# One layer of a hybrid encoder on one core: the seven products of an up-projection unit in a fixed order on TensorE

## The chip, the core and the metric

The kernel runs on one core of a Trainium2 chip. A core has five engines that run beside each other, each with a queue of its own: TensorE (matrix products; it writes to a memory of its own, PSUM, of eight banks), VectorE, ScalarE, GpSimd and SyncE (which issues most of the transfers). They wait for each other through semaphores. The metric is the time of one execution on the device in microseconds, lower is better.

## The reference

One layer works on 512 frames of a prompt and 64 frames of a sample, each a row of 2048 numbers. First come two recurrent mixers with their projections, then the feed-forward part, which is what matters here:

```python
def conv_ffn(h, st, w_up, ffn_conv_w, ffn_conv_b, w_down):
    gate, val = jnp.split(h @ w_up, 2, axis=-1)
    gate_c, new_st = causal_dwconv(gate, st, ffn_conv_w)
    act = jax.nn.silu(gate_c + ffn_conv_b) * val
    return act @ w_down, new_st
```

`w_up` is 2048 x 11264: 5632 gate columns and 5632 value columns. `causal_dwconv` is a convolution of width 3 along the frames. All arrays are float32.

## The kernel before

**The arithmetic.** A float32 product is made of three products of a shorter type: each weight block is split into `wh` (rounded, by ScalarE) and `wl` (the rest, by VectorE), each activation into `hi` and `lo`, and TensorE adds `wh*hi + wh*lo + wl*hi` in one PSUM bank.

**The up-projection.** It is cut into 44 units (`t`), each with 128 gate and 128 value columns. A unit is a 2 x 2 block product (gate and value by the two halves of the 2048 rows, against two halves of the frames), computed in Strassen's way with seven products (`c` = 0 to 6) in place of eight. The activations' combinations are made once, ahead of the stage. A product is 8 row blocks (`j`) times three matmuls of 128 x 128 weights by 290 columns: 24 matmuls into one bank (`up_product`, lines 1251 to 1263).

**The banks.** A unit takes a tile `g` of two banks and a tile `bank` of one (line 1255). The products go to x, y, z, x, y, z, y, where x and y are the banks of `g` and z is `bank`:

```python
        ps = self.banks[(0, 1, 2, 0, 1, 2, 1)[c]]
```

The products that come second and third to a bank add to what is there. Each product is read out as soon as it is done (`up_out`): c0 by ScalarE into `p1` (L1273); c1, c2, c3, c4 by VectorE (L1276, L1279, L1281, L1284); c5 and c6 by VectorE too (L1286 and L1287, L1291 and L1292).

**The weights.** `up_prep` prepares the weights of a product two products ahead: the sums that Strassen's way needs (`s1` L1219, `s2` L1228, L1238, L1243, 1.2 us each on VectorE) and the split (`wh` L1208 on ScalarE, `wl` L1209 on VectorE). Three pairs of split weights are kept, so a split begins when the product three before has released its pair. The raw blocks, 512 KB each, four a unit, come from DRAM by SyncE's queue into six buffers (`up_load`, L1202). After the gate's products its convolution runs on VectorE (L1311) and ScalarE (L1312), and the unit's result is multiplied (L1318) and written to DRAM (L1319). Two groups of VectorE's work, the convolution and the last multiplication, are already held behind the latest split with `issue_after`.

**The order.** No order of instructions is written out. The program is traced in the order of the loop in `up`, and a planner then runs it through a model of the engines: whenever an engine is free in the model, it issues the instruction that is ready there, the one traced first if there are several. What comes out is the fixed order of each engine's queue. `issue_after(ins)` adds an edge that holds for the order alone: what the block traces on `ins`'s engine is queued behind `ins`. It brings no semaphore.

Of the kernel before, what the change touches and what calls it, by code (L numbers as in the profile page):

```python
# [1 line left out]

# [1 line left out]

# [87 lines left out]
class Kern:  # L92
# [1158 lines left out]
    def up_product(self, t, c):  # L1251

        if c == 0:
            g = self.pgt()
            self.banks = g[:, 0, :HZ], g[:, 1, :HZ], self.bank()[:, :HZ]
        T, (wh, wl) = self.nc.tensor, self.a.pop((t, "w", c))
        ps = self.banks[(0, 1, 2, 0, 1, 2, 1)[c]]
        for j in range(NPAIR):
            hi, lo, _ = self.combos[c, j]

            T.matmul(ps, wh[:, j], hi, start=(c < 3 and j == 0), stop=False, skip_group_check=True)  # L1261
            T.matmul(ps, wh[:, j], lo, start=False, stop=False, skip_group_check=True)  # L1262
            T.matmul(ps, wl[:, j], hi, start=False, stop=(j == NPAIR - 1), skip_group_check=True)  # L1263

    def up_out(self, t, c):

        nc = self.nc
        V, A, G = nc.vector, nc.scalar, nc.gpsimd
        x, y, z = self.banks
        tmp = lambda n: self.ub.tile([P, HZ], F32, tag=n, name=self.name(n))  # L1270
        if c == 0:
            self.p1 = tmp("p1")
            A.activation(self.p1, x, AF.Copy)  # L1273
        elif c == 1:
            self.g = self.ub.tile([P, 2, HZ], F32, tag="g", name=self.name("g"))
            V.tensor_tensor(self.g[:, 1], y, self.p1, op=ALU.add)  # L1276
        elif c == 2:
            self.r = tmp("r")
            V.tensor_tensor(self.r, z, self.p1, op=ALU.add)  # L1279
        elif c == 3:  # L1280
            V.tensor_tensor(self.g[:, 0], x, self.rb[:, 0], op=ALU.mult)  # L1281
        elif c == 4:
            self.v = self.v_tile()
            V.tensor_tensor(self.v[:, 1], y, self.r, op=ALU.add)  # L1284
        elif c == 5:
            V.tensor_tensor(self.g[:, 1], z, self.g[:, 1], op=ALU.add)  # L1286
            V.tensor_tensor(self.g[:, 1], self.g[:, 1], self.rb[:, 1], op=ALU.mult)  # L1287
            self.up_gate(t, self.g)
        else:
            v = self.v  # L1290
            V.tensor_tensor(v[:, 0], y, self.p1, op=ALU.add)  # L1291
            V.tensor_tensor(v, v, self.rb, op=ALU.mult)  # L1292
# [33 lines left out]
    def up(self):  # L1326
        self.fs = self.cp.tile([P, 2, 2, NFF], F32, name="fs")
        self.cb = self.ub.tile([P, 2 * HZ], F32, tag="cb", name="cb")
        self.nc.gpsimd.tensor_copy(self.cb[:, 0:2], self.zero3[:, :2])
        self.up_state(0)  # L1330
        self.t2s = {}
        ahead = 2
        steps = [(t, c) for t in range(NFF) for c in range(7)]
        for n, (t, c) in enumerate(steps):
            if t == 0:
                for l in ((1,), (2,), (3,), (4,), (5, 6), (), ())[c]:
                    for j in range(N_EARLY, NPAIR):
                        self.pair_late(l, j)
            if n + ahead < len(steps):
                self.up_prep(*steps[n + ahead])  # L1340
            self.up_product(t, c)
            if n == 0:
                self.norm_end()

            if t > 0 and c == 0:
                with self.tc.issue_after(self.split_of):
                    self.up_conv(t - 1, self.ca)
                self.up_state(t)
            if t > 0 and c == 2:
                with self.tc.issue_after(self.split_of):  # L1350
                    self.up_act(t - 1, self.v, self.ca)
            self.up_out(t, c)
        self.up_conv(t, self.ca)
        self.up_act(t, self.v, self.ca)
# [291 lines left out]
```

## Time and profile before

| | us |
|---|---|
| median of 3 runs | 2995.6 (2995.07 to 3002.82) |
| the profiled execution | 3002.07 |
| its span, first to last instruction | 3000.3 |
| TensorE busy in the span | 2912.2 (97%) |
| VectorE busy | 2095.7 (70%) |
| ScalarE busy | 1242.9 (41%) |
| the up-projection, from its first matmul to its last | about 1020 |

How to read the rows further down. PE is TensorE, PEld its weight loads, DVE VectorE, ACT ScalarE, POOL GpSimd, SPq SyncE's queue. L1261 is line 1261 of the kernel. `g<-slot,wh` says that the instruction writes the tile `g` and reads the tiles `slot` and `wh`. A row of the timeline has the start, the duration, the engine, the line, the operation, the tiles, the shape, the count and, in brackets, the idle time of that engine before it and what ended it. A row of a window has its bounds and length, then the busy time and the number of instructions on PE, PEld, DVE, ACT and POOL (those engines that work in the windows asked for), the granted share of TensorE's clock, and the transfers' share and rate. Matmuls are pipelined: a row's duration is longer than the distance from one to the next.

### The profile page before, as it was taken

What the parts mean: (1) busy time and instruction counts of PE and PEld (TensorE: products, weight loads), DVE (VectorE), ACT (ScalarE), POOL (GpSimd) and SP (SyncE); (2) the same over time, 40 slices, a digit from 0 to 9 for tenths busy, and PEclk for the clock granted to TensorE, in tenths of its full rate; (3) what the DMA queues carried; (4) which work ended last, traced back from release to release, by engine and by line L of the source; (5) the groups of instructions that cost most, each with busy time, mean ns of one, the idle gap of its engine ahead of it and who ended that gap; (6) DMA issues with size and microseconds to landing.
All of it is one profiled execution on the core that took longest, in us unless ns stands there. A gap on an engine that the chain in (4) does not pass through costs nothing.

```text
span 3000.3 us, 52414 instructions
## 1 busy us (share of the span) xinstructions
PE 2912.2 (97%) x21128; PEld 2796.7 (93%) x21128; DVE 2095.7 (70%) x3226; ACT 1242.9 (41%) x2116; POOL 307.3 (10%) x610
## 2 busy tenths in 40 slices
PE   7988999999999999999999999999999999999998
PEld 3588899999999998999999999999999999999998
DVE  5776667776578777367888888888888865555555
ACT  6555444554343333255444444444444432212223
POOL 0033333332200000000000000000000000000000
PEclk9999999999999999999999999999999999999999
DMA  7844545554455456543333333333333473333221
GB/s 274 283 142 134 148 121 149 144 152 134 133 144 145 135 159 172 153 143 96 97 111 105 106 98 111 106 104 99 112 104 104 122 238 101 116 101 106 89 85 65
DMA packets 532599, 392.95 MB, mean 131 GB/s; under 512 B 58729, under 2 KB 463204, under 8 KB 532356
## 3 DMA queue, kind: packets, MB, share of 16 engines
q1 hardware_dynamic: 532356, 389.59, 43.5%
q8 instruction: 167, 2.74, 0.4%
q14 instruction: 76, 0.62, 0.1%
HBM read 355.16 MB, written 34.36 MB: 130 GB/s over the span
## 4 chain that ended last, share of the span: by engine, by line
PE 65%; DVE 2%; DMA 1%; ACT 1%; issue 1%; POOL 0%; SPq 0%; ACTq 0%; POOLq 0%; DVEq 0%
PE g L508 19%; PE g L510 10%; PE g L1261 8%; PE g L1262 8%; PE g L1263 8%; PE bank L1262 3%; PE bank L1261 3%; PE bank L1263 3%; PE bank L401 1%; DVE acc L738 0%; PE bank L140 0%; PE bank L744 0%; PE bank L1471 0%; POOL s L134 0%; DMA xr<-od 0%
## 5 line engine op out<-in xcount | busy, mean ns | idle before, releaser
L508 PE MATMUL g<-slot,wh 128*128 128x288 f32 x3168 | 551.9, 295 | 0.2 <-DVE slot L1031 0.2
L1261 PE MATMUL g<-slot,wh 128*128 128x290 f32 x1760 | 533.6, 303 | 2.4 <-ACT p L1273 2.4
L1262 PE MATMUL g<-slot,wh 128*128 128x290 f32 x1760 | 526.1, 299 | 0.0
L1263 PE MATMUL g<-slot,wl 128*128 128x290 f32 x1760 | 521.2, 296 | 0.0
L595 ACT ACTIVATE wh<-raw 128x1024 fp32r<-128x1024 f32 x223 | 235.4, 1058 | 613.6 <-PE g L508 596.7
L508 PEld LDWEIGHTS g<-slot,wh 128*128 128x128 f32 x3168 | 466.2, 188 | 0.7 <-DVE slot L1031 0.5
L508 PE MATMUL g<-hh,wh 128*128 128x288 f32 x1984 | 453.7, 307 | 1.9 <-DVE cb L881 1.5
L510 PE MATMUL g<-hh,wl 128*128 128x288 f32 x1984 | 443.9, 302 | 3.4 <-DVE wl L596 3.4
L508 PE MATMUL g<-hl,wh 128*128 128x288 f32 x1984 | 439.8, 301 | 0.0
L1031 DVE SCALAR_TENSOR_TENSOR slot<-g,mod,slot 128x512 f32<-128x512 f32 (+1 forms) x448 | 201.9, 492 | 308.9 <-PE g L510 304.7
L738 DVE SCALAR_TENSOR_TENSOR acc<-xr,ct,acc 128x512 f32<-128x512 f32 x480 | 340.0, 754 | 35.4 <-DMA xr<-in_w_ada_dram 34.8
L1208 ACT ACTIVATE wh<-raw 128x1024 fp32r<-128x1024 f32 x176 | 186.7, 1061 | 393.5 <-PE g L1262 389.1
L1261 PEld LDWEIGHTS g<-slot,wh 128*128 128x128 f32 x1760 | 331.1, 188 | 16.7 <-ACT p L1273 11.5
L510 PE MATMUL g<-slot,wl 128*128 128x288 f32 x1584 | 343.2, 295 | 0.0
L1263 PEld LDWEIGHTS g<-slot,wl 128*128 128x128 f32 x1760 | 336.5, 191 | 0.0
L1262 PEld LDWEIGHTS g<-slot,wh 128*128 128x128 f32 x1760 | 334.6, 190 | 0.1
L508 PEld LDWEIGHTS g<-hh,wh 128*128 128x128 f32 x1984 | 324.3, 191 | 5.7 <-issue 1.6
L510 PEld LDWEIGHTS g<-hh,wl 128*128 128x128 f32 x1984 | 324.8, 191 | 4.3 <-DVE wl L596 3.7
L508 PEld LDWEIGHTS g<-hl,wh 128*128 128x128 f32 x1984 | 324.7, 191 | 1.0 <-issue 0.7
L596 DVE TENSOR_TENSOR wl<-raw,wh 128x1024 fp32r<-128x1024 f32 x223 | 272.3, 1222 | 58.6 <-ACT wh L595 57.9
L510 PEld LDWEIGHTS g<-slot,wl 128*128 128x128 f32 x1584 | 254.9, 188 | 0.0
L1209 DVE TENSOR_TENSOR wl<-raw,wh 128x1024 fp32r<-128x1024 f32 x176 | 214.9, 1221 | 19.8 <-ACT wh L1208 19.3
(367 smaller groups left out, 4415.7 us busy)
## 6 DMA issues: line engine op xcount, KB each, us to landing
raw<-in_w_up_dram SPq DMA_DIRECT2D x176, 512.0 KB
xr<-in_w_ada_dram SPq DMA_DIRECT2D x128, 512.0 KB
raw<-in_w_in_dram SPq DMA_DIRECT2D x108, 512.0 KB
raw<-in_w_down_dram SPq DMA_DIRECT2D x88, 512.0 KB
hraw<-in_w_ada_dram SPq DMA_DIRECT2D x64, 512.0 KB
raw<-in_w_out_dram SPq DMA_DIRECT2D x32, 512.0 KB
slot<-actd SPq DMA_DIRECT2D x44, 288.0 KB
actd<-v SPq DMA_DIRECT2D x44, 256.0 KB
```

What stands on the lines that cost most here:

```text
L401: T.matmul(ps[:, b * 64:(b + 1) * 64], e3[:, b], qc[:, b * 64:(b + 1) * 64], start=True, stop=True)
L508: T.matmul(ps[:, h if bank is None else bank, :n], wh, x[:, h, :n], start=f, stop=False)
L510: T.matmul(ps[:, h if bank is None else bank, :n], wl, ah[:, h, :n], start=False, stop=stop)
L595: nc.scalar.activation(hi[:, :n_], raw[:, :n_], AF.Copy)
L596: nc.vector.tensor_tensor(lo[:, :n_], raw[:, :n_], hi[:, :n_].bitcast(F32), op=ALU.subtract)
L738: V.scalar_tensor_tensor(acc[s], w[:, k], col, acc[s], op0=ALU.mult, op1=ALU.add)
L1031: self.nc.vector.scalar_tensor_tensor(x1[:, :, z], ps[:, :, c], gain[:, q:q + 1], x1[:, :, z], op0=ALU.mult, op1=ALU.add)
L1208: self.nc.scalar.activation(hi, src, AF.Copy)
L1209: self.nc.vector.tensor_tensor(lo, src, hi.bitcast(F32), op=ALU.subtract)
L1261: T.matmul(ps, wh[:, j], hi, start=(c < 3 and j == 0), stop=False, skip_group_check=True)
L1262: T.matmul(ps, wh[:, j], lo, start=False, stop=False, skip_group_check=True)
L1263: T.matmul(ps, wl[:, j], hi, start=False, stop=(j == NPAIR - 1), skip_group_check=True)
```

## The change

The first matmul of every product is queued behind the last matmul of the product traced before it. `self.mm_last` holds that last matmul, from one product to the next and from one unit to the next.

```diff
-from contextlib import ExitStack
+from contextlib import ExitStack, nullcontext
...
         for j in range(NPAIR):
             hi, lo, _ = self.combos[c, j]
 
-            T.matmul(ps, wh[:, j], hi, start=(c < 3 and j == 0), stop=False, skip_group_check=True)
+            with self.tc.issue_after(self.mm_last) if j == 0 and self.mm_last else nullcontext():
+                T.matmul(ps, wh[:, j], hi, start=(c < 3 and j == 0), stop=False, skip_group_check=True)
             T.matmul(ps, wh[:, j], lo, start=False, stop=False, skip_group_check=True)
             T.matmul(ps, wl[:, j], hi, start=False, stop=(j == NPAIR - 1), skip_group_check=True)
+        self.mm_last = self.nc.cur_bb.bb.instructions[-1]
...
         self.up_state(0)
-        self.t2s = {}
+        self.t2s, self.mm_last = {}, None
         ahead = 2
```

## The prediction

> **What bounds the kernel now.** I read the page first (shares, then the slices), then one window over the whole up-projection, then what its first matmul line waits for, and last one unit instruction by instruction.
>
> ```profile
> span 3000.3 us, 52414 instructions
> PE 2912.2 (97%) x21128; PEld 2796.7 (93%) x21128; DVE 2095.7 (70%) x3226; ACT 1242.9 (41%) x2116; POOL 307.3 (10%) x610
> ```
> ```profile
> 1394.40:2414.60 1020.20, 1017.78 (x7411) 1002.88 (x7409) 839.51 (x1042) 460.53 (x554) 72.40 (x134) 1.00 0.38 109
> ```
> The last row is the up-projection: 44 units of seven products of 24 matmuls, 7392 of them, in 1020.2 us, TensorE busy 1017.8 of it at full clock. VectorE and ScalarE have a fifth and a half of the stage free, so TensorE alone sets its length, and any time it stands still is added to the end.
>
> Where does it stand still? Below: what ScalarE's copy of the first product (`p1`, L1273) makes others wait.
>
> ```profile
> L1273 ACT ACTIVATE p<-g x44: 391/395/397, 1400.6 to 2395.3; 128x290 f32<-128x290 f32 x44
>   PEld g L1261: 11.5, 43
>   PE g L1261: 2.4, 2
> ```
> The lines under it give idle time in us and how often. Now unit 18 on TensorE and ScalarE. I write c0 to c6 for the products. c0, c1, c3, c4 and c6 go to the tile `g` (c0 and c3 to its bank x, c1, c4 and c6 to its bank y), c2 and c5 to `bank`.
>
> ```profile
> 1818.17 0.30 PE L1263 MATMUL g<-slot,wl 128*128 128x290 f32 x1
> ...
> 1818.31 0.30 PE L1261 MATMUL bank<-slot,wh 128*128 128x290 f32 x1
> ...
> 1818.37 1.06 ACT L1208 ACTIVATE wh<-raw 128x1024 fp32r<-128x1024 f32 x1 [2.17 <-PE g L1262]
> ...
> 1819.34 0.39 ACT L1273 ACTIVATE p<-g 128x290 f32<-128x290 f32 x1
> ...
> 1819.51 0.29 PE L1261 MATMUL bank<-slot,wh 128*128 128x290 f32 x1
> ...
> 1819.79 0.41 PE L1261 MATMUL g<-slot,wh 128*128 128x290 f32 x1
> ...
> 1820.03 0.30 PE L1262 MATMUL g<-slot,wh 128*128 128x290 f32 x1
> ```
> c0 issues its last matmul at 1818.17. Ten matmuls of c2 follow, and only then c1, at 1819.79: 0.06 us after `p1` ended (1819.34 + 0.39). So c1, which writes y, waits for a copy that reads x. `p1` itself stands behind a 1.06 us weight split on ScalarE that c0's end also releases. The planner knows this wait and has put c2 into it. The same happens at c4, which waits for VectorE's reading of c3 (L1281):
>
> ```profile
> 1805.07 0.30 PE L1263 MATMUL g<-slot,wl 128*128 128x290 f32 x1
> 1805.21 0.30 PE L1261 MATMUL bank<-slot,wh 128*128 128x290 f32 x1
> ...
> 1805.75 0.30 PE L1262 MATMUL bank<-slot,wh 128*128 128x290 f32 x1
> 1805.92 0.40 PE L1261 MATMUL g<-slot,wh 128*128 128x290 f32 x1
> ```
> ```profile
> 1805.41 0.46 DVE L1281 TENSOR_TENSOR g<-g,sqa 128x290 f32<-128x290 f32 x1 [0.58 <-PE g L1263]
> ```
> c3's last at 1805.07, five matmuls of c5, c4 at 1805.92, which is 0.05 us after L1281 ended. In every unit looked at, the fill is ten and five:
>
> ```profile
> 1449.50:1450.90 1.40, 1.33 (x10) 1.33 (x10) 0.00 (x0) 0.00 (x0) 1.00 0.00 0
> 2325.30:2326.70 1.40, 1.33 (x10) 1.33 (x10) 0.00 (x0) 0.00 (x0) 1.00 0.00 0
> 1459.45:1460.10 0.65, 0.59 (x5) 0.65 (x5) 0.00 (x0) 0.00 (x0) 1.00 1.10 351
> 2335.25:2335.90 0.65, 0.59 (x5) 0.65 (x5) 0.00 (x0) 0.00 (x0) 1.00 1.11 351
> ```
> (These rows count the instructions on `bank` alone, in an early and a late unit.) The order on TensorE is thus c0, 10 of c2, c1, 14 of c2, c3, 5 of c5, c4, 19 of c5, c6.
>
> **The change, part by part.** It adds no instruction. It adds an order: each product's first matmul may be issued only behind the last one of the product before. The other 23 add to the same bank and follow their first.
>
> *Step 1, the fill before c1 goes.* c1 still can't start before `p1` is done. Nothing ahead of `p1` changes: c0's end releases the split, then the copy. So c1 still starts 1.62 us after c0's last issue, but TensorE does nothing in between, and behind c1's waiting matmul everything else of TensorE is queued. The ten matmuls are done later, at the spacing of (1805.75 - 1805.21) / 4 = 0.135 us: +1.35 us a unit. In the first unit the copy comes later still and two rows of the waits above (2.4 us) are mostly its own; there nothing was filled. 43 x 1.35 = **58 us**. The price from below: if `p1` goes ahead of the split, c1 starts like c4 does after its reader, 0.34 + 0.39 + 0.05 = 0.78 us after c0 (0.34 is 1805.41 - 1805.07). From above: one more ScalarE operation of the split's size ahead of it, 1.62 + 1.06 = 2.7 us. I take 1.62, because the release that puts the split first lies before the change.
>
> *Step 2, the fill before c4 goes.* In the same way +5 x 0.135 = 0.675 us, in 44 units: **30 us**.
>
> *Step 3, VectorE's order ahead of c4.* c3 now ends later against the work around it, so I place it, in the times of unit 18. c1 runs from 1819.79 to its last issue at 1820.03 + 22 x 0.135 = 1823.0, as now. c2 whole: 1823.13 to 1826.23. c3: 1826.37 to 1829.47, and L1281 can read it 0.34 us later, at 1829.81. What lies on VectorE there now:
>
> ```profile
> 1824.29 1.23 DVE L1209 TENSOR_TENSOR wl<-raw,wh 128x1024 fp32r<-128x1024 f32 x1 [0.43 <-ACT wh L1208]
> ...
> 1826.66 1.22 DVE L1209 TENSOR_TENSOR wl<-s,wh 128x1024 fp32r<-128x1024 f32 x1
> 1828.46 0.46 DVE L1281 TENSOR_TENSOR g<-g,sqa 128x290 f32<-128x290 f32 x1 [0.58 <-PE g L1263]
> 1829.82 1.23 DVE L1228 TENSOR_TENSOR s<-s,raw 128x1024 f32<-128x1024 f32 x1 [0.90 <-DMA raw<-in_w_up_dram]
> 1830.96 1.22 DVE L1209 TENSOR_TENSOR wl<-raw,wh 128x1024 fp32r<-128x1024 f32 x1
> ```
> ```profile
>   DMA raw<-in_w_up_dram: 35.4, 42
> ```
> ```profile
> 1825.54 0.37 SPq L1202 DMA_DIRECT2D raw<-in_w_up_dram  x1
> 1828.32 1.06 ACT L1208 ACTIVATE wh<-raw 128x1024 fp32r<-128x1024 f32 x1 [2.12 <-PE g L1262]
> ```
> L1228 (the next unit's s2) waits for a block in 42 units (the single row, 35.4 us of idle VectorE). Here SyncE asks for it at 1825.54, when the `wl` at 1824.29 has freed its buffer, and it lands 4.28 us later. The planner puts L1228 ahead of the `wl` at 1830.96, whose `wh` is ready at 1829.38: so it believes in a landing before 1829.4. It doesn't put it into the 0.58 us of idle time ahead of L1281: so it believes in one after about 1828.4. The load's own release hangs on c1 and doesn't move. In the new order the `wl` of 1826.66 moves with c2's end, 1.35 us, to 1828.0 to 1829.2; VectorE is then free until L1281 is ready at 1829.81, and the planner's landing falls just there. It will put L1228 **ahead** of L1281. On the chip the block lands at 1829.82 as before, L1228 holds VectorE until the next can start 1.14 us on (1830.96 - 1829.82), L1281 runs at 1830.96, and c4 starts 0.51 us later, at 1831.47, not at 1829.81 + 0.51 = 1830.32. That is +1.15 us in the 43 units that have a next one: **49 us**. If the planner decides otherwise it is 0; the upper bound is one more 1.22 us operation, 54 us.
>
> *What stays free.* c2 and c5 need no reader of `g`. c3 waits for the reader of c1 and c6 for that of c4, each now with a whole bank product (24 x 0.135 = 3.2 us) between, against 0.5 us of reading; VectorE's 839.5 of 1020.2 us leave room. Weight splits run three products ahead: `wh` and `wl` take 1.06 + 1.22 us of the 6.4 us until they are used. Without that cover the splits would cost up to 2.3 us a product.
>
> *Sum.* 58 + 30 + 49 = **137 us**, on the profiled execution's 3002.07 us (1.8 us over its span; the median of the runs is 2995.6, 6.5 lower). On the median: 2995.6 + 137 = **3133 us**, +4.6%.
>
> **The rivals.** *A. L1281 keeps its place* (step 3 is nothing): the planner's times need only be 0.4 us off the chip's for it. 2995.6 + 88 = **3084**. For it: the margin is small. Against: L1228 waited for its load in 42 units, so the planner always believes in an earlier landing than the chip's, and that puts L1228 first.
>
> *B. `p1` goes ahead of the split*: 0.84 us a unit less at c1, 36 us: 3097 with step 3, **3048** without. Against: at 1818.37 ScalarE had stood idle for 2.17 us and the split was free first.
>
> *C. Not slower.* The wait goes by bank and not by tile: x and y are two banks, so no c1 would need `p1`, and no c4 L1281. Then the strict order costs nothing, and today's leftovers go too: c1 starts 0.14 us late (1819.79 - 1819.51 - 0.135) and its second matmul 0.11 (0.24 - 0.135); c4 0.04 and 0.11. Together 0.40 x 44 = 17 us: **2978**. The point that decides is whether c1's start follows `p1`'s end, and the rows above speak against it, in 43 waits. [...]
>
> *D. The order changes nothing*, because the planner meets it in another way: 2996. Against: ten and five matmuls of another bank stand ahead of c1 and c4 in the rows.
>
> *E. The stalls also cost clock.*
>
> ```profile
> 811.59:815.00 3.41, 2.05 (x17) 1.85 (x16) 1.97 (x4) 0.00 (x0) 0.00 (x0) 1.00 0.82 234
> 815.00:818.41 3.41, 3.41 (x18) 3.40 (x16) 0.00 (x0) 0.38 (x1) 0.00 (x0) 0.50 1.06 327
> 333.71:337.13 3.42, 1.76 (x14) 1.73 (x15) 0.00 (x0) 1.80 (x5) 1.17 (x2) 1.00 0.50 136
> 337.13:340.54 3.41, 3.41 (x28) 3.41 (x28) 2.21 (x4) 1.24 (x2) 0.00 (x0) 1.00 0.96 242
> ```
> A 3.41 us stretch with TensorE busy for 2.05 is followed by one at half clock (0.50); another, busy for 1.76, is not. The longest new stall, from c3's end at 1829.77 to 1831.47, leaves 3.41 - 1.70 = 1.71. One half-clock stretch loses half of 3.41, 1.7 us; in each unit, 75 us: **3208**. [...]
>
> **How the numbers follow.** The forecast, all three steps: 0.48. A 0.22, B 0.14, E or one more operation ahead of a copy 0.08, C 0.03, D 0.05. The range takes in the forecast, A, and B from 3048 on, and above it step 1's upper bound (2.7 - 1.62 = 1.08 us in 43 units, 3133 + 46 = 3179), which also holds half of E's loss: **3050 to 3180**. What a measurement of this kernel can tell from no change is about 0.3%, 9 us. Slower: 0.48 + 0.22 + 0.14 + 0.08 = 0.92; same 0.05; faster 0.03.
>
> **What will show it.** Step 1: the waits of L1261 on L1273 grow from 13.9 us to 43 x 1.3 = 56 or more, and no `bank` matmul stands between c0 and c1. Step 2: L1281 appears as a releaser of L1261 in 44 units. Step 3: L1228 stands ahead of L1281, and those waits are 1.7 us each, not 0.55 (A). The stage grows from 1020 to about 1157 us and all else keeps its length. The forecast is wrong if c1 starts on c0's heels (C), if the copy precedes the split (B), or if the clock in the stage falls below 1.00 (E).

## The result and the profile after

The changed kernel takes **3147.8 us** (median, 3141.39 to 3155.57) against 2995.34 us before (2992.52 to 3002.82) in the same comparison: ratio **1.0506**, 95% interval 1.0476 to 1.0536. It is slower by 152 us; 3133 was forecast, with a range of 3050 to 3180. The profiled execution took 3155.57 us. First the head of the page after, then the row of one window over the whole up-projection:

```profile
span 3153.8 us, 52417 instructions
PE 2934.3 (93%) x21128; PEld 2813.3 (89%) x21128; DVE 2106.9 (67%) x3226; ACT 1243.3 (39%) x2116; POOL 303.1 (10%) x610
```
```profile
1391.20:2568.30 1177.10, 1040.98 (x7411) 1021.36 (x7411) 851.17 (x1043) 460.89 (x556) 72.88 (x134) 0.98 0.33 95
```

The stage grew from 1020.2 to 1177.1 us, 156.9 more. That accounts for the difference: what lies ahead of the stage became 3 us shorter (its first matmul stands at 1391 instead of 1394), and what follows it kept its length. TensorE's idle time in the stage is length less busy time: 136.1 us where it was 2.4. But its busy time rose as well, by 23.2 us, for the same 7392 matmuls, and the granted clock is 0.98 instead of 1.00. So there are two losses: standing still, and running slowly.

What TensorE waits for (who waited for `p1`, now on L1275, and for the reading of c3, now on L1283; idle time in us, how often):

```profile
L1275 ACT ACTIVATE p<-g x44: 391/395/396, 1397.4 to 2547.2; 128x290 f32<-128x290 f32 x44
...
  PE g L1262: 57.8, 44
...
L1283 DVE TENSOR_TENSOR g<-g,sqa x44: 451/453/460, 1410.4 to 2557.6; 128x290 f32<-128x290 f32 x44
...
  PE g L1264: 0.7, 1
...
  PE g L1262: 77.9, 44
```

Both readings now hold a product's first matmul (L1262) in each of the 44 units: 1.3 us each for `p1`, 1.8 us each for the reading of c3. The line between says that VectorE was idle just ahead of the reading only once: it came from other work. The timeline of a unit shows from which. Here c0 ends and c1 starts:

```profile
1985.81 0.30 PE L1264 MATMUL g<-slot,wl 128*128 128x290 f32 x1
1986.01 1.06 ACT L1208 ACTIVATE wh<-raw 128x1024 fp32r<-128x1024 f32 x1 [2.18 <-PE g L1263]
...
1986.97 0.40 ACT L1275 ACTIVATE p<-g 128x290 f32<-128x290 f32 x1
...
1987.42 0.40 PE L1262 MATMUL g<-slot,wh 128*128 128x290 f32 x1 [1.31 <-ACT p L1275]
```

And here c3 ends and c4 starts:

```profile
1995.20 1.23 DVE L1209 TENSOR_TENSOR wl<-s,wh 128x1024 fp32r<-128x1024 f32 x1 [0.55 <-ACT wh L1208]
...
1997.07 0.29 PE L1264 MATMUL g<-slot,wl 128*128 128x290 f32 x1
...
1997.30 1.23 DVE L1228 TENSOR_TENSOR s<-s,raw 128x1024 f32<-128x1024 f32 x1 [0.87 <-DMA raw<-in_w_up_dram]
1998.44 0.45 DVE L1283 TENSOR_TENSOR g<-g,sqa 128x290 f32<-128x290 f32 x1
...
1999.04 0.37 PE L1262 MATMUL g<-slot,wh 128*128 128x290 f32 x1 [1.69 <-DVE g L1283]
```

c1 starts 1.61 us after c0's last issue, as it did before, with nothing in between. c4 starts 1.97 us after c3's: VectorE sat 0.87 us waiting for a block of the next unit, did L1228 with it, and only then read c3. That is the order that step 3 of the prediction worked out. In the trace L1228 of the next unit runs ahead of the reading of c3 in 42 of the 43 units that have a next one; in the kernel before it does so in none.

The slow running, in four windows of one length, the first two from this unit, the others 27.3 us on:

```profile
1996.14:1999.56 3.42, 1.73 (x14) 1.53 (x13) 2.55 (x4) 1.06 (x1) 0.00 (x0) 1.00 0.36 108
1999.56:2002.97 3.41, 3.41 (x27) 3.41 (x27) 2.03 (x3) 0.55 (x1) 0.00 (x0) 1.00 0.15 40
2023.45:2026.86 3.41, 1.63 (x13) 1.62 (x13) 3.33 (x4) 1.00 (x1) 0.00 (x0) 0.99 0.01 2
2026.86:2030.27 3.41, 3.41 (x16) 3.41 (x16) 0.56 (x2) 0.28 (x1) 0.00 (x0) 0.51 0.48 137
```

The window with TensorE busy for 1.63 us is followed by one at half clock, in which 16 matmuls go instead of 27; the window with 1.73 us is not. There are 14 such half-clock stretches in the stage, where there was one before; all but the first follow a stall at c4. Each loses about (27 - 16) x 0.135 = 1.5 us; 13 more of them make 19.5.

### The profile page after: what moved, and what is told of

It reads as the page before. It is cut to its first block, busy times and chain, and to the rows that moved or that the text cites. A ratio compares the mean times of both kernels' runs of the same rounds, so it can differ in the third digit from the quotient of the medians.

```text
span 3153.8 us, 52417 instructions
## 1 busy us (share of the span) xinstructions
PE 2934.3 (93%) x21128; PEld 2813.3 (89%) x21128; DVE 2106.9 (67%) x3226; ACT 1243.3 (39%) x2116; POOL 303.1 (10%) x610
## 4 chain that ended last, share of the span: by engine, by line
PE 53%; DMA 6%; DVE 5%; ACT 3%; issue 2%; POOL 0%; SPq 0%; ACTq 0%; DVEq 0%; POOLq 0%
PE g L508 19%; PE g L510 9%; PE g L1262 7%; PE g L1263 6%; PE g L1264 6%; DMA raw<-in_w_up_dram 6%; DVE wl L1209 2%; PE bank L1263 2%; PE bank L1262 2%; PE bank L1264 2%; ACT wh L1208 2%; DVE s L1228 1%; DVE g L1283 1%; ACT p L1275 1%; PE bank L401 1%
## 5 line engine op out<-in xcount | busy, mean ns | idle before, releaser
L1262 PE MATMUL g<-slot,wh 128*128 128x290 f32 x1760 | 540.2, 307 | 135.7 <-DVE g L1283 77.9
L1263 PE MATMUL g<-slot,wh 128*128 128x290 f32 x1760 | 534.7, 304 | 0.0
L1264 PE MATMUL g<-slot,wl 128*128 128x290 f32 x1760 | 529.3, 301 | 0.0
L1262 PEld LDWEIGHTS g<-slot,wh 128*128 128x128 f32 x1760 | 339.6, 193 | 154.7 <-ACT wh L1208 69.4
L508 PEld LDWEIGHTS g<-slot,wh 128*128 128x128 f32 x3168 | 466.1, 188 | 0.7 <-DVE slot L1031 0.5
L1264 PEld LDWEIGHTS g<-slot,wl 128*128 128x128 f32 x1760 | 345.0, 196 | 0.0
L1263 PEld LDWEIGHTS g<-slot,wh 128*128 128x128 f32 x1760 | 342.9, 195 | 0.1
L510 PEld LDWEIGHTS g<-slot,wl 128*128 128x128 f32 x1584 | 254.9, 188 | 0.0
```

The costliest lines, as they stand in the source:

```text
L508: T.matmul(ps[:, h if bank is None else bank, :n], wh, x[:, h, :n], start=f, stop=False)
L510: T.matmul(ps[:, h if bank is None else bank, :n], wl, ah[:, h, :n], start=False, stop=stop)
```

## The experiments

Each time is a median, with the ratio to the kernel before in the same comparison (2995.3 us for the change, 2999.8 to 3002.7 us for the other runs). Stage, busy and idle are of TensorE in the up-projection of the profiled execution. The names of the products are those of the prediction.

| kernel | us | ratio, 95% interval | stage | busy | idle |
|---|---|---|---|---|---|
| before | 2995.3 | 1 | 1020.2 | 1017.8 | 2.4 |
| the change | 3147.8 | 1.0506 (1.0476 to 1.0536) | 1177.1 | 1041.0 | 136.1 |
| edge at c2 alone | 3097.8 | 1.0320 (1.0305 to 1.0336) | 1117.4 | 1021.1 | 96.3 |
| edge at c5 alone | 3030.3 | 1.0100 (1.0087 to 1.0113) | 1050.4 | 1019.6 | 30.8 |
| change, sums held | 3089.2 | 1.0287 (1.0269 to 1.0304) | 1108.0 | 1021.1 | 86.9 |
| change, copy first | 3156.7 | 1.0515 (1.0492 to 1.0539) | 1173.9 | 1064.0 | 109.9 |
| change, both of these | 3053.0 | 1.0173 (1.0152 to 1.0194) | 1071.9 | 1019.4 | 52.5 |
| change, two tiles | 3001.2 | 0.9996 (0.9985 to 1.0008) | 1020.8 | 1006.6 | 14.2 |
| before, two tiles | 2997.3 | 0.9987 (0.9975 to 1.0000) | 1016.8 | 1004.8 | 12.0 |
| before, two tiles, sums held | **2978.5** | 0.9921 (0.9907 to 0.9934) | 998.3 | 998.2 | 0.1 |
| change, two tiles, sums held | 2982.9 | 0.9937 (0.9923 to 0.9950) | 999.5 | 998.5 | 1.0 |
| before, sums held | 3001.2 | 0.9996 (0.9984 to 1.0007) | 1021.4 | 1018.8 | 2.6 |

**One part of the change alone.** Of the prediction's three steps, step 1 is the edge at c2 (which keeps c2 behind c1) and step 2 the edge at c5. The question was whether they add up, and where step 3 belongs.

```diff
-            with self.tc.issue_after(self.mm_last) if j == 0 and self.mm_last else nullcontext():
+            with self.tc.issue_after(self.mm_last) if j == 0 and self.mm_last and c in (2,) else nullcontext():
```

> The order is added at c2 alone (c2 behind c1); c4 may still overtake c5. My theory: the fill before c1 goes, 43 x 1.35 = 58 us; and since c3 then ends later, L1228 goes ahead of L1281 here too, and c4 starts about 2.0 us after c3's last issue instead of 0.85, with 7 matmuls of c5 in between where there were 5: 43 x 0.9 = 39 us. Together 3092, a few us more if the clock drops somewhere (3085 to 3110). Rival (the terms are apart and VectorE's order belongs to c5's edge): 2995 + 58 = 3053.

```diff
-            with self.tc.issue_after(self.mm_last) if j == 0 and self.mm_last else nullcontext():
+            with self.tc.issue_after(self.mm_last) if j == 0 and self.mm_last and c in (5,) else nullcontext():
```

> The order is added at c5 alone (c5 behind c4); c1 may still overtake c2. My theory: c3 ends where it ended before, L1281 stays ahead of L1228, only the five matmuls before c4 go: 44 x 0.675 = 30 us, 3025 (3020 to 3032), no half-clock stretch. Rival (terms apart, VectorE's order belongs to c5's edge): 3025 + 50 = 3075.

Measured: +97 us of stage with c2's edge, +30 with c5's. The reading of c3, for c2's edge and then for c5's. Lines with L1264 say how long VectorE stood idle ahead of it until c3's last matmul, the line with L1262 how long c4's first matmul then waited for the reading:

```profile
L1283 DVE TENSOR_TENSOR g<-g,sqa x44: 451/453/461, 1415.2 to 2503.3; 128x290 f32<-128x290 f32 x44
...
  PE g L1264: 1.0, 1
...
  PE g L1262: 37.8, 42
```
```profile
L1283 DVE TENSOR_TENSOR g<-g,sqa x44: 452/459/461, 1405.9 to 2427.6; 128x290 f32<-128x290 f32 x44
...
  PE g L1264: 24.5, 42
```

With c5's edge VectorE stands ready and waits for TensorE in 42 units, so the reading is on time and only the fill is lost: 30 us, as step 2 has it. With c2's edge it comes from other work, as in the changed kernel. So the late reading comes with c2's edge and not with c5's, and its 37.8 us of waits at c4 account for what c2's edge costs beyond the 58 us of its fill (97 - 58 = 39).

**L1228 held behind the reading.** This takes step 3 away and leaves the order of the products. L1238, which is held with L1228, works on the same block of the next unit.

```diff
-            V.tensor_tensor(s2, g("s1"), g("a11"), op=ALU.subtract)
+            with self.tc.issue_after(self.x_read) if self.x_read else nullcontext():
+                V.tensor_tensor(s2, g("s1"), g("a11"), op=ALU.subtract)
...
-            V.tensor_tensor(g("a21"), g("a11"), g("a21"), op=ALU.subtract)
+            with self.tc.issue_after(self.x_read) if self.x_read else nullcontext():
+                V.tensor_tensor(g("a21"), g("a11"), g("a21"), op=ALU.subtract)
...
             V.tensor_tensor(self.g[:, 0], x, self.rb[:, 0], op=ALU.mult)
+            self.x_read = self.nc.cur_bb.bb.instructions[-1]
...
```

> The changed kernel, with the two sums that wait for the next unit's a11 block (L1228 and L1238) queued behind the reading of c3 (L1281) on VectorE. My theory: c4 starts 0.85 us after c3's last issue again instead of 2.06, which takes off 53 us, and the half-clock stretches of the stage, some 15 us, go with the long stalls: 3080 (3075 to 3092). If the clock is tripped by the stalls at c1 too, it stays at 3095. Rival (c4 waits for something else than the reading of c3): 3148.

The reading of c3 in this kernel, and its stage:

```profile
L1285 DVE TENSOR_TENSOR g<-g,sqa x44: 460/460/461, 1413.6 to 2491.8; 128x290 f32<-128x290 f32 x44
...
  PE g L1266: 41.2, 43
...
  PE g L1264: 28.4, 44
```
```profile
1394.40:2502.40 1108.00, 1021.14 (x7411) 1001.53 (x7410) 851.17 (x1042) 460.63 (x555) 73.12 (x134) 1.00 0.35 101
```

VectorE now waits for c3 (41.2 us in 43 units), L1228 comes behind the reading in every unit, and c4 waits 28.4 us in all instead of 77.9. Against the changed kernel TensorE's idle time falls by 136.1 - 86.9 = 49.2 us and its busy time by 1041.0 - 1021.1 = 19.9: the clock is at 1.00 again. So holding two sums gives back both, the late reading and the slow stretches, and what remains, 1108.0 - 1020.2 = 87.8 us, is steps 1 and 2.

**The copy ahead of the split.** The reserve that rival B had pointed to, taken on purpose: c3's split goes behind `p1` on ScalarE.

```diff
-    def up_split(self, src):
+    def up_split(self, src, behind=None):
...
-        self.nc.scalar.activation(hi, src, AF.Copy)
+        with self.tc.issue_after(behind) if behind else nullcontext():
+            self.nc.scalar.activation(hi, src, AF.Copy)
...
-            w = self.up_split(g("a12"))
+            w = self.up_split(g("a12"), self.p1_ins)
...
             A.activation(self.p1, x, AF.Copy)
+            self.p1_ins = self.nc.cur_bb.bb.instructions[-1]
```

> The changed kernel, with c3's weight split queued behind the copy p1 on ScalarE. My theory: c1 starts 0.78 us after c0's last issue instead of 1.61: 43 x 0.83 = 36 us less, 3112 (3105 to 3118), and the half-clock stretches stay, since the long stalls at c4 make them. Rival (c1's stall makes them): about 3097. Rival (the split is on the path itself, and is late for c3 when it stands second): no gain, 3148.

This missed: 3156.7 us, no gain. The place itself did what was expected. c1 now starts 0.80 us after c0's last issue, 0.81 less than in the changed kernel, and TensorE's idle time fell by 136.1 - 109.9 = 26.2 us (less than 43 x 0.81 = 34.8, since c4's waits on the reading of c3 grew from 77.9 to 86.4). But busy time rose by 1064.0 - 1041.0 = 23.0. Three windows of this kernel, each with the one behind it:

```profile
1775.77:1779.18 3.41, 1.55 (x12) 1.35 (x11) 2.40 (x3) 1.06 (x1) 0.00 (x0) 1.00 0.28 83
1779.18:1782.59 3.41, 3.41 (x16) 3.41 (x16) 1.46 (x2) 0.00 (x0) 0.00 (x0) 0.50 0.18 52
1803.07:1806.49 3.42, 0.79 (x7) 0.59 (x6) 1.98 (x3) 1.06 (x1) 0.00 (x0) 1.00 0.15 39
1806.49:1809.90 3.41, 3.41 (x16) 3.41 (x16) 1.88 (x2) 0.00 (x0) 0.00 (x0) 0.50 0.05 11
1830.38:1833.79 3.41, 1.45 (x11) 1.25 (x10) 2.26 (x4) 1.06 (x1) 0.00 (x0) 1.00 0.32 96
1833.79:1837.21 3.42, 3.42 (x17) 3.42 (x16) 1.67 (x2) 0.00 (x0) 0.00 (x0) 0.50 0.11 30
```

The stage has 30 such stretches instead of 14, nine of them in a row at 27.3 us from each other. 27.3 us is eight windows of 3.41. From c3's last matmul to the next unit's it takes 27.1 us (median) where a slow stretch lies between and 25.3 where none does. 27.1 is 0.2 short of eight windows, so from such a unit to the next the stall moves by 0.2 us against the windows. In the changed kernel the same two are 27.8 and 26.1, there it moves by 0.5, and the longest row is three. That the stall's place in its window is what makes the rows is the author's estimate from these numbers; no run isolates it.

**Both edits.** This run was planned before the miss was known, but it bears on it: if the clock took the copy's gain, the gain must appear once c4's long stalls are gone.

> Both holds together in the changed kernel. My theory: stalls of 0.78 us at c1 and 0.85 us at c4 alone are left, no half-clock stretch in the stage: 3148 - 53 - 36 - 15 = 3044 (3038 to 3052). If the terms hide each other, more.

Measured 3053.0, 1 us above the range expected, in a comparison whose kernel before stood 4.5 us above 2995.3. The stage:

```profile
1393.00:2464.90 1071.90, 1019.40 (x7412) 999.37 (x7411) 851.23 (x1043) 460.95 (x556) 72.18 (x134) 1.00 0.36 105
```

The granted clock is 1.00 in it, c4's waits on the reading of c3 are 28.5 us in all, busy time is 1019.4 and idle time 52.5: against the run with the sums held alone, 34.4 us less idle time, where 43 x 0.81 = 34.8 was to be had. So the copy ahead of the split is worth its full 34 us. In the run with the copy first alone the slower clock took 23.0 of them and c4's longer waits 8.5; the stage was left 3 us shorter, which the medians don't show.

**Two tiles.** Rival C said that c1 need not wait for a reading of x, because x and y are two banks. Here they become two tiles. Each is the first bank of a tile of two banks, and the second bank of each stays unused: a unit now takes both buffers of the pool, where one unit used to take the one and the next unit the other. First in the changed kernel, then in the kernel before:

```diff
-            g = self.pgt()
-            self.banks = g[:, 0, :HZ], g[:, 1, :HZ], self.bank()[:, :HZ]
+            self.banks = self.pgt()[:, 0, :HZ], self.pgt()[:, 0, :HZ], self.bank()[:, :HZ]
```

> The changed kernel, with x and y taken as two tiles of one bank each instead of one tile g of two banks; nothing else is changed. My theory (a product that writes y waits for the reading of x only because both lie in one tile): c1 no longer waits for p1 nor c4 for L1281, the strict order costs nothing and the leftovers of 0.40 us a unit go: 2978 us (2972 to 2986), no wait of the first matmuls on p1. Rival (strict order itself is what costs, whatever the waits): about 3148, as the changed kernel.

> The kernel before, with x and y as two tiles, no order added. My theory: nothing has to be filled any more, so the planner issues the seven products one behind the other by itself, and the time is that of the changed kernel with two tiles, within 4 us: 2978 (2972 to 2986). Rival (the wait on p1 comes from elsewhere, the weights or the planner): 2995, with c2 still cut into 10 and 14.

Measured 3001.2 and 2997.3: neither differs from the kernel before by what can be told. The first half of the expectation held. With two tiles the strict order costs at most the 4 us between these two runs, so the 152 us all hang on one thing: in this kernel a wait goes by the tile, not by the bank. One unit of the strict run, with c0's last matmul, c1's first, and the copy:

```profile
1819.45 0.30 PE L1263 MATMUL g<-slot,wl 128*128 128x290 f32 x1
...
1819.59 0.30 PE L1261 MATMUL g<-slot,wh 128*128 128x290 f32 x1
...
1820.62 0.40 ACT L1274 ACTIVATE p<-g 128x290 f32<-128x290 f32 x1
1820.67 0.29 PE L1263 MATMUL g<-slot,wl 128*128 128x290 f32 x1
```

With x and y in different tiles TensorE writes y while ScalarE reads x in this run (from 1820.62 on, above), c1 starts ahead of the copy's end in all 44 units, and the waits on `p1`, 57.8 us in 44 units, are gone. In the free order the planner now issues the seven products whole from the second unit on, one behind the other, without being told to.

The second half of the expectation, a gain of 17 us, failed. In the strict run of the two, L1228's wait in VectorE's queue, and then one unit on VectorE and TensorE:

```profile
L1228 DVE TENSOR_TENSOR s<-s,raw x44: 1217/1225/1227, 1214.6 to 2383.1; 128x1024 f32<-128x1024 f32 x44
...
  DMA raw<-in_w_up_dram: 121.5, 42
```
```profile
1738.73 1.23 DVE L1228 TENSOR_TENSOR s<-s,raw 128x1024 f32<-128x1024 f32 x1 [5.16 <-DMA raw<-in_w_up_dram]
1739.87 0.45 DVE L1282 TENSOR_TENSOR g<-g,sqa 128x290 f32<-128x290 f32 x1
1740.24 1.22 DVE L1238 TENSOR_TENSOR raw<-raw,raw 128x1024 f32<-128x1024 f32 x1
1741.37 1.22 DVE L1209 TENSOR_TENSOR wl<-raw,wh 128x1024 fp32r<-128x1024 f32 x1
1742.51 0.45 DVE L1285 TENSOR_TENSOR v<-g,r 128x290 f32<-128x290 f32 x1
```
```profile
1739.89 0.30 PE L1263 MATMUL bank<-slot,wl 128*128 128x290 f32 x1
1743.11 0.37 PE L1261 MATMUL g<-slot,wh 128*128 128x290 f32 x1 [2.92 <-DVE v L1285]
```

VectorE stands still for 5.16 us at L1228, and everything behind it is late: the reading of c3 (L1282), then that of c4 (L1285), which c6 needs because it writes c4's bank. L1228 waits 121.5 us in all, where it waited 35.4 in the kernel before. That points at the same two sums on VectorE as what took the gain of TensorE's better order back; the next runs test it.

**Two tiles and the sums held.** If so, the sums' edit of above should bring the 17 us out. It was put on the free order (held behind the reading of c3) and on the strict one (behind the reading of c4).

> The kernel before with x and y in two tiles of one bank each (the edit of the free order run), and with L1228 and L1238, the two sums that wait for the next unit's a11, put on VectorE behind the reading of c3. In the run with the two tiles alone the waits of c1 and c4 were gone, but c6 waited for the reading of c4 in some 20 units by 0.3 to 3.3 us, 17.2 us in all, and the time stood at 2997. Theory: that reading was late because the two sums stood ahead of it on VectorE and waited for a landing. Then the waits on the reading of c4 go and the 17 us of the two tiles come out: about 2981 (2977 to 2988), the stage at 1003 instead of 1016.6. Rival: late landings cost their time wherever the sums stand, since the parts of s2 for the next unit's c1 come from them; then the gaps in front of c1 and c4 of the next unit grow to the same 17 us and the time stays at 2997 (2994 to 3001).

> The changed kernel with x and y in two tiles of one bank each, and with L1228 and L1238 put on VectorE behind the reading of c4. Its order on TensorE is that of the run above, so both theories expect the same of it as of that run: about 2981 (2977 to 2988) if the late sums were what kept the gain of the two tiles away, 2997 to 3001 if not. If the two runs differ by over 4 us, the order on TensorE itself has a price that the strict run with two tiles alone (3001) did not show.

2978.5 and 2982.9 us: **faster than both kernels**, by 0.8% and 0.6% against the one before. The free one, L1228's waits (its line is L1229 there) and the stage:

```profile
L1229 DVE TENSOR_TENSOR s<-s,raw x44: 1215/1218/1227, 1216.5 to 2362.3; 128x1024 f32<-128x1024 f32 x44
...
  DMA raw<-in_w_up_dram: 6.0, 8
```
```profile
1395.00:2393.30 998.30, 998.16 (x7410) 997.38 (x7409) 844.45 (x1042) 460.23 (x555) 73.36 (x134) 1.00 0.39 112
```

The sum waits in 8 units for 6.0 us, where it waited in 42 units in each of the two runs with two tiles alone (121.5 us in the strict one, 113.3 in the free one), and TensorE is busy 998.16 of 998.30 us. The two runs differ by 4.4 us, just over the 4 that the expectation named, but their stages by 1.2 only and their intervals overlap: a price of the order itself isn't shown.

**The sums held in the kernel before**, behind the reading of c4, x and y in one tile: does the gain need the two tiles?

> The kernel before, x and y in the one tile g as they are, and only L1228 and L1238 put on VectorE behind the reading of c4. It tells whether the 21 us gained with both edits come from the sums alone. Theory: in the kernel before, the 17 us are lost at c1 and c4 (0.40 us a unit, each starting just after a reading of the other bank), and the sums were late for nobody there, so holding them alone gives nothing: 2998 (2994 to 3003) on a before of 2998 to 3002, ratio 0.998 to 1.002. Rival: the late sums cost time in the kernel before too, and the tile nothing; then the time is about 2980, ratio 0.993.

3001.2 us, no change. Neither edit gains alone: the tile keeps TensorE waiting where the sums are in time, and the sums keep it waiting where x and y are in two tiles. (The sums stand one reading later here than in the free run of two tiles, which held them behind the reading of c3.)

## Why the prediction was right, point by point

**What bounds.** Right: TensorE set the stage, and every stall went to the end.

**Steps 1 and 2, the fills.** Forecast 58 + 30 = 88 us. With the sums held the change costs 87.8 us of stage, and c5's edge alone 30.2. Right, and the place too: c1's start after c0 didn't move (1.61 us), the ten matmuls did.

**Step 3, VectorE's order.** Forecast 49 us from L1228 going ahead of the reading of c3. It went there in 42 of 43 units, and undoing it takes 49.2 us of idle time away. Right in size and cause; rival A falls. That it comes with c2's edge and not with c5's was in the working (c2's later end is what moves the `wl`), but not drawn out.

**The term that was missed** is the clock. The sum had it at nothing, the author's estimate, and left it to rival E at 75 us, as if it must come in every unit or in none. There are 14 slow stretches for 44 units, and they cost 19.9 us. That is the difference between the 137 us of the forecast and the 157 of the stage: 87.8 + 49.2 + 19.9 = 156.9. The prediction had named a clock below 1.00 in the stage as a sign that it is wrong, and the clock fell to 0.98: in this term it was wrong, and the time stayed within the range because its upper end had left room for half of E's loss. Of the two pairs of windows that the prediction showed for E, the busier (2.05) is the one with half clock behind it, so they set no limit; and its own figure, 1.71 us busy beside the longest stall, lay where unit 22 (1.73, full clock) and the next (1.63, half) differ. A cost that could as well come as not, by these numbers, belonged in the sum with a share of its price, and not in a rival with 0.08.

**Rivals.** B didn't happen by itself; done on purpose, the copy ahead of the split is worth 34.4 us of idle time and 36.1 of the stage, where 36 were forecast, if the clock stays up. C's mechanism doesn't hold for this program as it stands, where the waits on `p1` grew to 57.8 us; with x and y in two tiles these waits are gone, and the strict order costs at most 4 us. Its price of 17 us came only when the sums were held as well (998.3 against 1020.2 us, 22 us). D falls: the order on TensorE changed as forecast.

## What to carry to other kernels

Where an order fixes which product goes next, ask what each product's first write waits for, by tile and not by bank: here a reading of one bank of a shared tile held the write to the other (57.8 us of waits on `p1` in 44 units), and with the banks in two tiles it did not. Price a stall on TensorE twice, once as idle time and once for the clock behind it: in this stage the stalls at c4 were 77.9 us of waits, and the half-clock stretches, all but one behind such a stall, cost 19.9 us more. And when a gain that the busy rows promise doesn't come, look on the other engines for an instruction that waits for a transfer with the urgent one queued behind it; here two sums that stood too early cost 18.5 us of the stage in one kernel (two tiles, free order) and, with the clock, 69 us in another (the change).

## What was not expected of the hardware

In the trace of the changed kernel the half-clock stretches begin on a fixed grid of 3.413 us (to within 0.005 us). I laid that grid over its stage and over that of the run with the copy first, and added up TensorE's busy time in each window. (The windows shown further up begin 0.07 us behind it, hence their 0.99 and 0.51.) In the first, 13 of the 14 windows ahead of a slow stretch had it busy for 1.65 us or less, and the first of all, at c1's stall in the first unit, for 1.84; of the windows followed by full clock, the lowest had 1.60, the next 1.66. In the second, all 30 had 1.64 us or less, and the lowest of the others 1.64. None of the 14 was idle throughout: the least busy had 0.79 us. In the run with c2's edge alone all windows but one have it busy for 2.06 us or more, and none of these was followed by half clock; the one, in the first unit, had 1.17 us, and was. These are counts of this stage and no limit: in earlier stages of the kernel before, the window at 811.59 was followed by half clock with 2.05 us busy, and the one at 378.10 with 3.41, so busy throughout; why is open.
